# Moving the tiles of a decoder kernel to other bytes of the partition: parts of weights, keys and values at byte 64 modulo 128, parts of activations at byte 0

## The chip, the cores and the metric

The kernel runs on one core of a Trainium2 chip. The metric is the device time of one execution in microseconds. Three runs of the kernel before took 1002.29, 1002.46 and 1003.86 us; their median, 1002.46 us, is the time to compare with.

## The reference

A trunk of two layers works on 256 tokens of width 1024, all in float32. Each layer is a mixer between two half-step SwiGLU blocks, with an RMS norm ahead of every part and one at the end:

```python
y = (silu(h @ w_gate) * (h @ w_up)) @ w_out                    # SwiGLU, four times; D_FF = 2816
u, v = split(gelu(h @ w_in)); y = (u * (W_s @ LN(v) + b)) @ w_out   # mixer of layer 0; width 2048
y = stick_breaking_attention(h @ w_q, k, v) @ w_o              # mixer of layer 1; 16 heads of 64
```

Keys and values (4 heads) are projected once, from the output of layer 0. Every product is a product of a weight with 256 columns of activations, and every weight is read from memory once.

## The kernel before, in words

Float32 accuracy is kept by splitting each operand of a product into two parts, a high one of type float32r and the low rest. `mm3` (lines 144 to 150) then issues three matmuls for each tile of 128x128 weights: low weight by high activation (L148), high weight by low activation (L149), high by high (L150). A matmul has a stationary operand of 128 columns, which is loaded into the array (LDWEIGHTS, PEld in the profile), and a moving operand, which streams past it. The load for a matmul goes on while the matmul ahead of it streams.

`Weights.run_to` loads a weight tile of 128x1024 (`raw`, L71), splits it on ScalarE (`whi`, L81) and VectorE (`wlo`, L83), and hands it on some steps later. The steps follow in program order on TensorE:

- In a SwiGLU block, tagged a, b, c, d in order, step `in j` makes two banks, `g` and `u`, of 48 matmuls each. The weight is stationary and `xnh`, `xnl` (the normalised activations) move, 256 columns. Step `out j` adds 48 matmuls to four banks `y`: weight stationary, `hh`, `hl` (the gated hidden parts) moving. There are 11 steps of each kind in a block, and `out` comes one or two steps behind `in`. In block d, `out` is turned round: `hh`, `hl` are stationary and the weight moves, 512 columns (bank `yo`).
- The mixer of layer 0 has `v` (weight moving, `xn` stationary), `uu` (like `in`), `mix` (plain float32) and `ys` (like `out`).
- The attention has `kT` and a second `v` from `xkh`, `xkl`; `q` from `xn`; `z` (keys `kz` moving, `qh`, `ql` stationary); `o` (values `vd` stationary, `a0`, `a1` moving); and `yo` with `oT` moving.

Between the steps stand short float32 matmuls: the norm's `columns` (L313) and `rows` (L327), and transposes (`pgain` L253, `xb` L819).

A tile's byte in the partition follows from the order in which the pools are opened. They lie one behind the other, and each slot is rounded up to 32 bytes. In `const` the one-column tile `eps` takes 32 bytes; the pool ends at byte 18976, which is 32 modulo 128. `act` follows with `xT`, `xnh`, `xnl`, `acc` (multiples of 128 bytes, so all at 32), `rT` (32 bytes) and `spare` (2572 bytes in 2592), which leaves 96 for `rawp`, `hip`, `lop` and `hp`: `raw`, `whi`, `wlo`, `hh`, `hl`, `a0`, `a1` and `qh`, `ql` all start at 96. Slices of these tiles step by multiples of 512 bytes, so a tile's place modulo 128 holds for every operand cut from it. The pool `att` opens at 0: `kz`, `vd`, `xkh`, `xkl` and `oT` (in the slots of `xkh`, `xkl`) are at 0.

Of the kernel before, what the change touches and what calls it, by code (L numbers as in the profile page):

```python
# [8 lines left out]
F32 = mybir.dt.float32  # L9
# [6 lines left out]
P = 128  # L16
T = 256
# [82 lines left out]
def trunk(  # L100
# [21 lines left out]
    x = x[0]  # L122
    out = out[0]

    const = ctx.enter_context(tc.tile_pool(name="const", bufs=1))
    act = ctx.enter_context(tc.tile_pool(name="act", bufs=1))
    rawp = ctx.enter_context(tc.tile_pool(name="rawp", bufs=7))
    hip = ctx.enter_context(tc.tile_pool(name="hip", bufs=9))
    lop = ctx.enter_context(tc.tile_pool(name="lop", bufs=9))
    hp = ctx.enter_context(tc.tile_pool(name="hp", bufs=4))  # L130
    scr = ctx.enter_context(tc.tile_pool(name="scr", bufs=8))
    small = ctx.enter_context(tc.tile_pool(name="small", bufs=3))
# [131 lines left out]
    acc = act.tile([P, T], F32, name="acc")  # L264
    rT = act.tile([P, 2], F32, name="rT")

    spare = act.tile([P, P + 1 + 2 * (T + 1)], F32, name="spare")
    rb = spare[:, :T]
    diag = spare[:, T : 2 * T].rearrange("p (n t) -> p n t", n=2)

# [18 lines left out]
            nc.scalar.activation(s, xT[:, d, :], AF.Square)  # L289
            nc.gpsimd.tensor_add(acc, acc, s)  # L290

    eps = const.tile([P, 1], F32, name="eps")
    nc.vector.memset(eps, RMS_EPS)

    def newton(o, root, v, w):
# [343 lines left out]

    att = ExitStack()  # L640
    at = att.enter_context(tc.tile_pool(name="att", bufs=1))
    kz = [at.tile([P, 4, 2, T], F32R, name=f"kz{p}") for p in "hl"]
    vd = [at.tile([P, 2, 4, 2, 64], F32R, name=f"vd{p}") for p in "hl"]
    xkh = at.tile([P, KC, T], F32R, tag="bigh", name="xkh")
    xkl = at.tile([P, KC, T], F32R, tag="bigl", name="xkl")
    for t in kz:
# [265 lines left out]
```

## Time and profile before

| | |
|---|---|
| median of 3 runs | 1002.46 us |
| profiled execution, its own time | 1004.4 us |
| its span, first to last instruction | 1002.7 us |
| TensorE busy / loads of weights busy | 982.3 us / 963.5 us |
| VectorE / ScalarE / GpSimd busy | 645.2 / 504.1 / 86.5 us |
| traffic from memory | 176.73 MB read, 177 GB/s over the span |

Matmuls overlap in the pipeline: the busy time of one (its "mean ns") is more than twice the distance from its start to that of the next. The pace of TensorE is read from starts, as the time between two instructions divided by the matmuls between them.

### The profile page before, as it was taken

Reading aid. Unit: us, or ns where it says so; the run is one execution under the profiler, and the core shown is the slowest. Engines: PE = TensorE matmul, PEld = TensorE weight load, DVE = VectorE, ACT = ScalarE, POOL = GpSimd, SP = SyncE. Lnnn points to the kernel's source line nnn. Section 1 sums busy time; section 2 is a strip of 40 time slices with the busy share of each in tenths; the row PEclk is TensorE's granted clock in tenths of the full one; section 3 lists DMA queues with packets and bytes.
Section 4 is the critical chain, followed back from the end, with each engine's and each line's share of the span. In section 5 each row is a group of like instructions: output and inputs, shape, how many; then the busy total and the mean of one; then the engine's idle time right before and its main releaser. Section 6 shows DMA issues by size and latency. Waiting matters only on the chain.

```text
span 1002.7 us, 19306 instructions
## 1 busy us (share of the span) xinstructions
PE 982.3 (98%) x8042; PEld 963.5 (96%) x8042; DVE 645.2 (64%) x823; ACT 504.1 (50%) x690; POOL 86.5 (9%) x126
## 2 busy tenths in 40 slices
PE   8999999999999999999999999999997899999996
PEld 8999999999999999999999999999997899999996
DVE  6864675675866775656569755555678775565644
ACT  6643434475544564444448444444487674444433
POOL 4000000020000300000003000000046320000002
PEclk9999999999999999999999999999999999999999
DMA  9966565647555455666564866665643346656511
GB/s 304 322 195 190 169 189 188 190 143 222 184 177 175 133 191 188 193 188 193 186 195 146 247 189 191 189 193 186 190 149 92 97 147 191 207 172 203 176 42 43
DMA packets 135208, 179.56 MB, mean 179 GB/s; under 512 B 5624, under 2 KB 119376, under 8 KB 135120
## 3 DMA queue, kind: packets, MB, share of 16 engines
q1 hardware_dynamic: 134768, 177.76, 56.7%
q8 instruction: 63, 1.03, 0.4%
q0 software_dynamic: 192, 0.52, 0.2%
q14 instruction: 25, 0.20, 0.1%
q10 hardware_dynamic: 160, 0.05, 0.0%
HBM read 176.73 MB, written 1.05 MB: 177 GB/s over the span
## 4 chain that ended last, share of the span: by engine, by line
PE 89%; DVE 5%; ACT 2%; issue 1%; DMA 1%; POOL 1%; SPq 0%; ACTq 0%; POOLq 0%; DVEq 0%
PE yo L148 2%; PE yo L150 2%; PE yo L149 2%; PE yb L148 2%; PE yb L150 2%; PE yb L149 2%; PE ud L148 2%; PE ud L150 2%; PE gd L148 2%; PE ud L149 2%; PE gb L148 2%; PE gd L150 2%; PE gd L149 2%; PE ub L148 2%; PE gc L150 2%; PE gb L150 2%
## 5 line engine op out<-in xcount | busy, mean ns | idle before, releaser
L81 ACT CAST whi<-raw 128x1024 fp32r<-128x1024 f32 (+1 forms) x333 | 342.7, 1045 | 391.0 <-issue 205.3
L83 DVE TENSOR_TENSOR wlo<-raw,whi 128x1024 fp32r<-128x1024 f32 (+1 forms) x333 | 402.1, 1225 | 200.9 <-ACT whi L81 200.0
L290 POOL TENSOR_TENSOR acc<-acc,sq 128x256 f32<-128x256 f32 x39 | 33.8, 867 | 387.5 <-ACT sq L289 385.6
L148 PE MATMUL ga<-xnh,wlo 128*128 128x256 f32 x176 | 50.1, 285 | 0.0
L148 PE MATMUL ya<-hha,wlo 128*128 128x256 f32 x176 | 49.9, 284 | 0.2 <-DVE xT L399 0.2
L148 PE MATMUL yc<-hhc,wlo 128*128 128x256 f32 x176 | 49.9, 284 | 0.1
L148 PE MATMUL yb<-hhb,wlo 128*128 128x256 f32 x176 | 49.9, 284 | 0.0
L149 PE MATMUL ga<-xnl,whi 128*128 128x256 f32 x176 | 49.3, 280 | 0.5 <-DVE xnl L277 0.5
L149 PE MATMUL ya<-hla,whi 128*128 128x256 f32 x176 | 49.7, 282 | 0.0
L148 PE MATMUL gd<-xnh,wlo 128*128 128x256 f32 x176 | 49.7, 282 | 0.0
L149 PE MATMUL yb<-hlb,whi 128*128 128x256 f32 x176 | 49.7, 282 | 0.0
L149 PE MATMUL yc<-hlc,whi 128*128 128x256 f32 x176 | 49.7, 282 | 0.0
L150 PE MATMUL yb<-hhb,whi 128*128 128x256 f32 x176 | 49.6, 283 | 0.0
L148 PE MATMUL ua<-xnh,wlo 128*128 128x256 f32 x176 | 49.1, 279 | 0.5 <-DVE wlo L83 0.5
L150 PE MATMUL ya<-hha,whi 128*128 128x256 f32 x176 | 49.4, 283 | 0.0
L150 PE MATMUL gd<-xnh,whi 128*128 128x256 f32 x176 | 49.4, 281 | 0.0
L150 PE MATMUL ud<-xnh,whi 128*128 128x256 f32 x176 | 49.4, 281 | 0.0
L148 PE MATMUL ud<-xnh,wlo 128*128 128x256 f32 x176 | 49.4, 281 | 0.0
L149 PE MATMUL ud<-xnl,whi 128*128 128x256 f32 x176 | 49.4, 281 | 0.0
L149 PE MATMUL gd<-xnl,whi 128*128 128x256 f32 x176 | 49.4, 281 | 0.0
L150 PE MATMUL yc<-hhc,whi 128*128 128x256 f32 x176 | 49.4, 283 | 0.0
L150 PE MATMUL ga<-xnh,whi 128*128 128x256 f32 x176 | 49.1, 279 | 0.0
(289 smaller groups left out, 3353.6 us busy)
## 6 DMA issues: line engine op xcount, KB each, us to landing
raw<-in_ffn_w_in_dram SPq DMA_DIRECT2D x176, 512.0 KB, 4.5
raw<-in_ffn_w_out_dram SPq DMA_DIRECT2D x88, 512.0 KB, 4.3
raw<-in_a_w_in_dram SPq DMA_DIRECT2D x32, 512.0 KB, 4.4
raw<-in_a_w_out_dram SPq DMA_DIRECT2D x16, 512.0 KB, 3.3
raw<-in_b_w_q_dram SPq DMA_DIRECT2D x8, 512.0 KB, 4.5
raw<-in_b_w_o_dram SPq DMA_DIRECT2D x8, 512.0 KB, 4.0
raw<-in_w_kv_dram SPq DMA_DIRECT2D x4, 512.0 KB, 4.0
xin<-in_x_dram SPq DMA_DIRECT2D x4, 256.0 KB, 4.9
```

What stands on the lines that cost most here:

```text
L81: ins = nc.scalar.copy(hi[:, cc], raw[:, cc])
L83: ins = nc.vector.tensor_sub(lo[:, cc], raw[:, cc], hi[:, cc].bitcast(F32))
L148: nc.tensor.matmul(o, al, bh, start=first, stop=False, skip_group_check=True)
L149: nc.tensor.matmul(o, ah, bl, start=False, stop=False, skip_group_check=True)
L150: nc.tensor.matmul(o, ah, bh, start=False, stop=last, skip_group_check=True)
L290: nc.gpsimd.tensor_add(acc, acc, s)
```

## The change

The work and its order stay as they are. Only places move, by padding:

```diff
+    def gap(name, size):
+        pool = ctx.enter_context(tc.tile_pool(name=name, bufs=1))
+        pool.tile([P, size // 4], F32, name=f"{name}t")
     const = ...
     act = ctx.enter_context(tc.tile_pool(name="act", bufs=1))
+    gap("gapw", 32)
     rawp = ...; hip = ...; lop = ...
+    gap("gaph", 64)
     hp = ctx.enter_context(tc.tile_pool(name="hp", bufs=4))
...
-    spare = act.tile([P, P + 1 + 2 * (T + 1)], F32, name="spare")
+    spare = act.tile([P, P + 1 + 2 * (T + 1)], F32, name="spare", padded_shape=[P, 672])
-    eps = const.tile([P, 1], F32, name="eps")
+    eps = const.tile([P, 1], F32, name="eps", padded_shape=[P, 32])
...
     at = att.enter_context(tc.tile_pool(name="att", bufs=1))
+    at.tile([P, 8], F32, name="gapk")
     kz = ...; vd = ...
+    at.tile([P, 16], F32, name="gapx")
     xkh = ...; xkl = ...
```

Nothing reads or writes the gaps. By the sizes, the start bytes modulo 128 become:

| tiles | before | after |
|---|---|---|
| `xT`, `xnh`, `xnl`, `acc` | 32 | 0 |
| `spare` | 64 | 32 |
| `raw`, `whi`, `wlo` | 96 | 64 |
| `hh`, `hl`, `a0`, `a1`, `qh`, `ql` | 96 | 0 |
| `kz`, `vd` | 0 | 64 |
| `xkh`, `xkl`, `oT` | 0 | 0 |
| `wsT`, `bias`, `vsb`, `u` of the first mixer | 0 | 32 |

So the distance from the moving operand to the stationary one, modulo 128, goes from 64 to 64 where `xn` meets a weight, from 0 to 64 where `hh`, `hl` meet a weight, and from 32 or 96 to 64 in `kT`, the second `v`, `z`, `o` and the attention's `yo`.

## Rows read from the trace of the kernel before

**Rows 1.** The page: busy time by engine, and the granted clock by slices.
```profile
PE 982.3 (98%) x8042; PEld 963.5 (96%) x8042; DVE 645.2 (64%) x823; ACT 504.1 (50%) x690; POOL 86.5 (9%) x126
PEclk9999999999999999999999999999999999999999
```

**Rows 2.** The page: the chain that ended last, by engine.
```profile
PE 89%; DVE 5%; ACT 2%; issue 1%; DMA 1%; POOL 1%; SPq 0%; ACTq 0%; POOLq 0%; DVEq 0%
```

**Rows 3.** Timeline, block c: start us, us, engine, line, operation, out<-in, shapes, count.
```profile
572.57 0.29 PE L148 MATMUL gc<-xnh,wlo 128*128 128x256 f32 x1
...
583.47 0.28 PE L148 MATMUL yc<-hhc,wlo 128*128 128x256 f32 x1
...
589.21 0.29 PE L148 MATMUL gc<-xnh,wlo 128*128 128x256 f32 x1
```

**Rows 4.** Timeline, block d.
```profile
838.01 0.28 PE L148 MATMUL gd<-xnh,wlo 128*128 128x256 f32 x1
...
849.32 0.39 PE L148 MATMUL yo<-whi,hld 128*128 128x512 f32 x1
...
854.76 0.28 PE L148 MATMUL gd<-xnh,wlo 128*128 128x256 f32 x1
```

**Rows 5.** Groups by line and form: busy us, mean ns of one | idle us before.
```profile
L150 PE MATMUL gc<-xnh,whi 128*128 128x256 f32 x176 | 48.6, 276 | 0.0
L150 PE MATMUL gb<-xnh,whi 128*128 128x256 f32 x176 | 48.7, 277 | 0.0
L150 PE MATMUL ua<-xnh,whi 128*128 128x256 f32 x176 | 48.9, 278 | 0.0
L150 PE MATMUL uu<-xnh,whi 128*128 128x256 f32 x128 | 35.7, 279 | 0.0
L150 PE MATMUL v<-whi,xnh 128*128 128x256 f32 x128 | 35.8, 279 | 0.0
L150 PE MATMUL q<-xnh,whi 128*128 128x256 f32 x64 | 17.9, 279 | 0.0
L150 PE MATMUL gd<-xnh,whi 128*128 128x256 f32 x176 | 49.4, 281 | 0.0
L150 PE MATMUL yc<-hhc,whi 128*128 128x256 f32 x176 | 49.4, 283 | 0.0
L149 PE MATMUL ys<-hls,whi 128*128 128x256 f32 x128 | 36.2, 283 | 0.0
L149 PE MATMUL yo<-wlo,hhd 128*128 128x512 f32 x82 | 31.9, 389 | 0.0
```

**Rows 6.** Timeline, block a: a step behind a transpose of gains.
```profile
75.89 0.27 PE L253 MATMUL pgain<-ident,rows 56*128 56x56 f32 x1
76.08 0.39 PE L148 MATMUL ga<-xnh,wlo 128*128 128x256 f32 x1
76.31 0.28 PE L149 MATMUL ga<-xnl,whi 128*128 128x256 f32 x1
...
87.50 0.28 PE L148 MATMUL ya<-hha,wlo 128*128 128x256 f32 x1
```

**Rows 7.** Timeline, attention: one step of `yo`, up to the next `z`.
```profile
766.59 0.28 PE L148 MATMUL yo<-oTh,wlo 128*128 128x256 f32 x1
...
769.41 0.28 PE L148 MATMUL z<-kzh,ql 128*128 128x256 f32 x1
```

**Rows 8.** Timeline, block d: sixteen transposes in a row.
```profile
830.78 1.91 PE L819 MATMUL xb<-ident,xT 128*128 128x128 f32 x16
```

**Rows 9.** Groups by line and form: the splits of weights.
```profile
L83 DVE TENSOR_TENSOR wlo<-raw,whi 128x1024 fp32r<-128x1024 f32 x331 | 400.8, 1228 | 200.9 <-ACT whi L81 200.0
L81 ACT CAST whi<-raw 128x1024 fp32r<-128x1024 f32 x331 | 341.5, 1047 | 390.8 <-issue 205.3 <-PE gb L150 41.4 <-PE gd L150 39.4
```

## The prediction, made before the changed kernel ran

> **What bounds the kernel now.** I read the busy times first. TensorE is busy for 982.3 of 1002.7 us and its clock was granted in full in all 40 slices; no other engine is above 65% [rows 1]. Then the chain of waits: 89% of it is TensorE [rows 2]. So the end is set by how fast one matmul follows the other. The busy time can't tell this, since matmuls overlap, so I read starts in the timeline next. The reader is to see that one and the same matmul, 256 columns of float32r, runs at three paces.
>
> - In block c a step `in` has 96 matmuls from 572.57 to 583.47: 10.90 us, 113.5 ns each. The step `out` behind it has 48 up to 589.21: 5.74 us, 119.6 ns each [rows 3].
> - In block d the same step `in` takes 11.31 us for its 96: 117.8 ns each. The 24 wide matmuls (512 columns) behind it take 5.44 us: 226.7 ns each [rows 4].
>
> The groups by line repeat this over the whole run: the duration of one is the pace plus some 163 ns, so 276 ns stands for 113, 281 for 118, 283 for 120 [rows 5]. Nothing else separates these groups: the shape, the clock and the number of loads are the same. What differs between `in` (113.5 or 117.8) and `out` (119.6) is where the operands lie: moving at 32 and stationary at 96 in the one, both at 96 in the other. A step `in` has two paces at one and the same placing. The first of block c follows a step `out` and takes 113.5. A step that follows a lone transpose takes 87.50 - 76.31 = 11.19 us for 95 matmuls, 117.8 ns [rows 6], and keeps that to its end. I read this as two streams out of the same memory, the running operand and the next weights, that meet or miss each other; the distance modulo 128 says how often, and with a distance of 64 there are two rhythms, of which a break in the stream picks one.
>
> **The change part by part.** No instruction is added, removed or moved in its queue; no semaphore is added. The gaps are not written. What changes is the pace of three sets of matmuls.
>
> *Steps `out` of blocks a, b, c and `ys`.* Twelve groups, 9 x 176 + 3 x 128 = 1968 matmuls, now at 119.6 ns [rows 3, 5]. Their distance goes from 0 to 64, the distance that `in` has. They can then take either rhythm of `in`: at 117.8 each saves 1.8 ns (3.5 us in all), at 113.5 it saves 6.1 ns (12.0 us). I take the middle, 115.65 ns, since the groups of `in` are spread over both [rows 5]: 1968 x 3.95 = 7.8 us.
>
> *The wide matmuls of block d.* 3 x 82 = 246 at 226.7 ns, distance 0 [rows 4, 5]. No row shows a wide one at another distance in a steady stream. If a wide one loses per weight load what a narrow one loses, the gain is between nothing and 6.1 ns: 0 to 1.5 us. I take half, 0.8 us.
>
> *Attention, distance 32 or 96.* `yo` with `oT`: 24 matmuls in 2.82 us, 117.5 ns [rows 7]. There are 192 of these, 48 in `kT`, 48 in the second `v`, and 48 narrow ones in `z` and `o`: 336. At `yo`'s pace for all, going to 117.8 costs 0.1 us and going to 113.5 gains 1.3 us. Middle: 0.6 us.
>
> *Steps `in`, `uu`, `v`, `q`.* 24 groups of 176 and 15 rounds of 64 (`uu` 384, `v` 384, `q` 192): 5184 matmuls. Their distance stays 64, both operands move down by 32 bytes. I take nothing. The bounds are wide, since these are two thirds of the work. From (mean - 276) / 5 in the groups [rows 5], the share at 117.8 is about 0.5 in block a, 0.2 in b, 0 in c, 1 in d, 0.6 in `uu`, `v`, `q`: some 2300 matmuls. If all these went to 113.5 the gain is 2300 x 4.3 = 9.9 us; if the other 2900 went to 117.8 the loss is 12.5 us.
>
> *The small float32 matmuls and other engines.* Norm columns, rows, transposes and `mix` are under 300 instructions; sixteen transposes in a row run at (1.91 - 0.27) / 15 = 109 ns with the stationary operand at 32 and the moving one at 96 [rows 8]. I cost their shift at nothing. `raw`, `whi` and `wlo` move together, so the splits keep their relative places; they take 400.8 us of VectorE and 341.5 of ScalarE [rows 9], hidden under TensorE. That cover would be gone only if each grew by half. A faster TensorE asks for weights 1% sooner, which both can give.
>
> *Sum.* 7.8 + 0.8 + 0.6 + 0 = 9.2 us. The profiled execution took 1004.4 us (span 1002.7, 1.7 around it), so its like would take 995.2 us. It lies 1.9 us above the median of the runs; against the median, 1002.46 - 9.2 = 993.3 us.
>
> One rule of the Trainium skill speaks against any of this. The trace first: matmuls of one shape go at 113.5, 117.8 and 119.6 ns in neighbouring steps [rows 3, 4]. The page "TensorE: Matmul & The Clock Gate", section "Part 2: What happens when you issue a matmul", says that TensorE has two independent read ports, so that loading the next weights takes no read bandwidth from the running matmul. By that rule the place would not matter and the time would stay 1002.5 us; the rows disagree, unless the paces have a cause that I do not see (a rival below).
>
> **The rivals.**
>
> *Slower: the slow rhythm is carried on.* In the kernel before, a step `out` at distance 0 forces its own beat, and the `in` behind it came out at 113.5 [rows 3]. With one distance everywhere nothing resets the rhythm: what a norm or a transpose leaves behind [rows 6] holds through `in` and `out` until the next break. Price if it holds everywhere: 2900 x 4.3 = 12.5 us lost in `in`, 3.5 us won in `out`: 9.0 us more, 1011.5 us. It decides at the first steps behind a norm (the third step of block b: 113 or 118). For it: in block d, whose wide steps stand between, every `in` stays at 117.8 [rows 4, 5]. Against it: breaks differ, and block c is fast throughout [rows 5]. If it holds in one block only, gains and losses nearly cancel and the time is about 997.
>
> *The fast rhythm everywhere.* If 0 and 64 admit only the rhythm of 113.5: 12.0 + 9.9 + 1.5 + 1.3 = 24.7 us, 977.8 us. For it: 113.5 is the commonest pace at this distance. Against it: distance alone did not settle it in block d.
>
> *No meeting at all.* Both operands then start at a multiple of 64 bytes, which none but attention's tiles did. If runs of 64 bytes are what the memory hands out, a moving operand at 32 touches one run more than at 0, and 113.5 isn't the floor. The nearest row below is the transposes' 109.2 ns [rows 8]: 1968 + 5184 + 336 = 7488 matmuls gain a further 4.3 ns, 32 us beside the 24.7: 945.6 us. Against it: `oT` moves at 0, and its steps take 117.5 [rows 7], though at distance 32. In a sentence by itself: the same page of the Trainium skill, section "Back-to-back issue gap", gives 262 cycles for 256 columns, an estimate of 109.2 ns, which would make the same time.
>
> *The place as such matters the other way.* If 0 and 64 bring the pace of 119.6 to all: 2900 x 6.1 + 2300 x 1.8 = 21.8 us more, 1024.3 us. No row speaks for it; none excludes it, for no float32r pair at 0 and 64 is in the trace.
>
> *Nothing happens.* The paces come from something else that the blocks differ in, such as the bank written or the slices' higher address bits: 1002.5 us. Against it: the three blocks a, b, c agree on 119.6 in `out`, whatever slots they use.
>
> **How the numbers follow.** Forecast, a mixture of the two rhythms: 0.40, its own range 986 to 1000. Fast everywhere 0.20 (972 to 985); no meeting 0.15 (940 to 965); slow rhythm carried on 0.15 (1000 to 1012); nothing 0.06; worse everywhere 0.04. About 0.2% is what a measurement of this kernel can tell from no change. Faster by more: nearly all of the forecast, the two fast cases, a little of the carried rhythm, 0.73. Same: 0.09. Slower: most of the carried rhythm and the worst case, 0.18. The range from 950 to 1011 leaves out the lower part of the no-meeting case, the top of the carried one and the worst one, some 0.15 in all. Likeliest time 993.3 us.
>
> **What would show each step.** In the groups by line, `out` of a, b, c and `ys` should leave 283 ns: at 276 to 281 the distance is the cause, still at 283 the first step is wrong. Wide `yo` should fall from 389 to between 383 and 389. `gd` at 276 would speak for the fast rhythm everywhere, `gc` at 281 for the carried one; means of 272 to 273 in any of them for no meeting. Splits, loads and queues should keep their times. The forecast is wrong if steps `out` keep 119.6, or if `in`, which I left alone, moves by more than 9 us in all.

## The result and the profile after

The changed kernel takes 1011.33 us (median of four runs, 1010.14 to 1012.31) where the kernel before, run beside it, takes 1003.16: a ratio of 1.0079, interval 1.0060 to 1.0097. It is slower by 0.8%, where 0.9% faster was forecast. The time is that of the first rival, the slow rhythm carried on (1011.5 us).

The page of the profile after, busy times, granted clock and chain, which answer to [rows 1, 2]:

```profile
PE 992.0 (98%) x8042; PEld 972.0 (96%) x8042; DVE 643.9 (64%) x823; ACT 504.1 (50%) x690; POOL 85.5 (8%) x126
...
PEclk9999999999999999999999999999998999999999
...
PE 91%; DVE 4%; ACT 2%; DMA 1%; issue 1%; POOL 1%; SPq 0%; ACTq 0%; POOLq 0%; DVEq 0%
```

TensorE is busy 9.7 us longer for the same 8042 matmuls, at the same clock (2.4 GHz, full in all slices but one); VectorE, ScalarE and GpSimd moved by less than 2 us. So the loss is pace, as the sums from start to start below bear out. The groups by line and form of after, against [rows 5] (the lines of `mm3` are now L156 to L158):

```profile
L158 PE MATMUL gc<-xnh,whi 128*128 128x256 f32 x176 | 49.1, 279 | 0.0
...
L158 PE MATMUL v<-whi,xnh 128*128 128x256 f32 x128 | 35.4, 277 | 0.0
...
L158 PE MATMUL gd<-xnh,whi 128*128 128x256 f32 x176 | 49.2, 279 | 0.0
...
L158 PE MATMUL yc<-hhc,whi 128*128 128x256 f32 x176 | 48.8, 279 | 0.0
...
L157 PE MATMUL ys<-hls,whi 128*128 128x256 f32 x128 | 35.7, 279 | 0.0
...
L157 PE MATMUL yo<-wlo,hhd 128*128 128x512 f32 x82 | 32.3, 394 | 0.0
```

`gc` went up from 276 and `yc` down from 283, to one value. The reader should not take the mean's last digit for the pace (`gd` fell from 281 to 279 at the same pace); starts decide. The timeline of after in block c and in block d, answering to [rows 3, 4]:

```profile
574.67 0.28 PE L156 MATMUL gc<-xnh,wlo 128*128 128x256 f32 x1
...
585.98 0.28 PE L156 MATMUL yc<-hhc,wlo 128*128 128x256 f32 x1
...
591.63 0.28 PE L156 MATMUL gc<-xnh,wlo 128*128 128x256 f32 x1
...
844.08 0.28 PE L156 MATMUL gd<-xnh,wlo 128*128 128x256 f32 x1
...
855.39 0.39 PE L156 MATMUL yo<-whi,hld 128*128 128x512 f32 x1
...
860.99 0.28 PE L156 MATMUL gd<-xnh,wlo 128*128 128x256 f32 x1
```

Block c: 11.31 us for 96 matmuls of `in` (117.8 ns, before 113.5) and 5.65 us for 48 of `out` (117.7, before 119.6). Block d: `in` as before, 11.31 us; the 24 wide ones 5.60 us, 233.3 ns each, where they took 226.7. Summed from start to start over both whole traces:

| steps | before, us | after, us | change |
|---|---|---|---|
| `in` of a, b, c, d | 490.5 | 500.4 | +9.9 |
| `out` of a, b, c and `ys` | 238.0 | 234.5 | -3.6 |
| wide, block d | 56.0 | 57.5 | +1.5 |
| `uu` and `q` | 71.1 | 72.3 | +1.2 |
| both `v`, `kT`, `z`, `o`, narrow `yo` | 109.4 | 107.3 | -2.1 |
| float32 | 28.4 | 28.8 | +0.3 |

That is +7.3 us beside +6.8 in the spans (1002.7 to 1009.5).

### The profile page after: what moved, and what is told of

Its sections match the earlier page's. It is cut to its first block, busy times and chain, and to the rows that moved or that the text cites. A ratio compares the mean times of both kernels' runs of the same rounds, so it can differ in the third digit from the quotient of the medians.

```text
span 1009.5 us, 19306 instructions
## 1 busy us (share of the span) xinstructions
PE 992.0 (98%) x8042; PEld 972.0 (96%) x8042; DVE 643.9 (64%) x823; ACT 504.1 (50%) x690; POOL 85.5 (8%) x126
## 4 chain that ended last, share of the span: by engine, by line
PE 91%; DVE 4%; ACT 2%; DMA 1%; issue 1%; POOL 1%; SPq 0%; ACTq 0%; POOLq 0%; DVEq 0%
PE yo L156 2%; PE yo L158 2%; PE yo L157 2%; PE gc L156 2%; PE uc L156 2%; PE ub L158 2%; PE gb L158 2%; PE ud L156 2%; PE gc L158 2%; PE ub L157 2%; PE gb L157 2%; PE uc L158 2%; PE gb L156 2%; PE gd L156 2%; PE ub L156 2%; PE uc L157 2%
## 5 line engine op out<-in xcount | busy, mean ns | idle before, releaser
L156 PE MATMUL ga<-xnh,wlo 128*128 128x256 f32 x176 | 50.4, 286 | 0.0
L156 PE MATMUL ua<-xnh,wlo 128*128 128x256 f32 x176 | 49.4, 281 | 0.5 <-DVE wlo L83 0.5
L156 PE MATMUL yc<-hhc,wlo 128*128 128x256 f32 x176 | 49.5, 281 | 0.1
L156 PE MATMUL ya<-hha,wlo 128*128 128x256 f32 x176 | 49.5, 281 | 0.2 <-DVE xT L407 0.2
L156 PE MATMUL gd<-xnh,wlo 128*128 128x256 f32 x176 | 49.5, 281 | 0.0
L156 PE MATMUL gc<-xnh,wlo 128*128 128x256 f32 x176 | 49.5, 281 | 0.0
L156 PE MATMUL gb<-xnh,wlo 128*128 128x256 f32 x176 | 49.4, 281 | 0.0
L156 PE MATMUL yb<-hhb,wlo 128*128 128x256 f32 x176 | 49.4, 281 | 0.0
L158 PE MATMUL ga<-xnh,whi 128*128 128x256 f32 x176 | 49.3, 280 | 0.0
L156 PE MATMUL uc<-xnh,wlo 128*128 128x256 f32 x176 | 49.3, 280 | 0.0
L158 PE MATMUL gb<-xnh,whi 128*128 128x256 f32 x176 | 49.3, 280 | 0.0
L158 PE MATMUL ub<-xnh,whi 128*128 128x256 f32 x176 | 49.3, 280 | 0.0
L156 PE MATMUL ud<-xnh,wlo 128*128 128x256 f32 x176 | 49.2, 280 | 0.0
L158 PE MATMUL ua<-xnh,whi 128*128 128x256 f32 x176 | 49.2, 279 | 0.0
L158 PE MATMUL gd<-xnh,whi 128*128 128x256 f32 x176 | 49.2, 279 | 0.0
L156 PE MATMUL ub<-xnh,wlo 128*128 128x256 f32 x176 | 49.1, 279 | 0.0
L158 PE MATMUL ud<-xnh,whi 128*128 128x256 f32 x176 | 49.1, 279 | 0.0
```

The source lines that it names most:

```text
L156: nc.tensor.matmul(o, al, bh, start=first, stop=False, skip_group_check=True)
L158: nc.tensor.matmul(o, ah, bh, start=False, stop=last, skip_group_check=True)
```

## The experiments

Each kernel was timed beside the kernel before on the same chip, except the three bare streams, which ran once, with a profile. Bytes are places in the partition, worked out from the order and sizes of the tiles. Modulo 256 the distance (moving minus stationary) has a sign: in before it is 32 - 96, that is 192, in `in`, and 0 in `out`; in after it is 128 - 64 = 64 in both.

**h_at_64.** After, with the second gap behind `hp` and not ahead of it: h goes back to 64, `out` to distance 0, and `in` stays as in after.

```diff
-    gap("gaph", 64)
     hp = ...
+    gap("gaph", 64)
```

> The changed kernel with hh and hl (and a0, a1, qh, ql) at 64 in place of 0, all else in its new place. Carried rhythm (my theory): with distance 0 the steps out of blocks a, b, c take 119.6 to 120 ns again (group mean 283) and hand a fresh beat to the steps in, which go back to 113.3 ns in blocks b and c (276); the wide yo of block d back to 226.7 (389). About the time of the kernel before, 1000 to 1005 us. Rival, the place as such (0 and 64 slow, 32 and 96 fast): in stays at 117.8 (280) and out is at 120, some 1014 us. Rival, something else that the padding moved (scratch, norms): 1011 us, in at 117.8.

Measured: 1014.91 us, ratio 1.0105 (1.0091 to 1.0119). Block c:

```profile
578.61 0.28 PE L156 MATMUL gc<-xnh,wlo 128*128 128x256 f32 x1
...
589.92 0.29 PE L156 MATMUL yc<-hhc,wlo 128*128 128x256 f32 x1
...
595.68 0.28 PE L156 MATMUL gc<-xnh,wlo 128*128 128x256 f32 x1
```

`out` is back at 120 ns (5.76 us for 48) but `in` stays at 117.8 (11.31 for 96), in all 30 steps at 64 that follow one at distance 0 undisturbed; before has 28 such steps to 192, all fast. That a step `out` at distance 0 resets `in` to the fast rhythm fell as a general rule: it does so in before and not here, with the same distances modulo 128.

**h_only.** Before, with h alone moved by 64 bytes, from 96 to 32 modulo 128.

```diff
+    gap = ctx.enter_context(tc.tile_pool(name="gaph", bufs=1))
+    gap.tile([P, 16], F32, name="gapht")
     hp = ...
+    gap = ...                                  # "gaps", 64 bytes more
+    gap.tile([P, 16], F32, name="gapst")
     scr = ...
```

The second gap brings all that lies behind h to 128 bytes further on, the same place modulo 128.

> The kernel before with hh, hl, a0, a1, qh, ql alone moved, from 96 to 32, so that every pair of a weight and an activation is 64 apart, with x at 32 and weights at 96 as before. Carried rhythm: the same loss as with the whole change, in of blocks b and c at 117.8 (280), out at 117.8 (280), wide yo 233 (394): 1007 to 1013 us. Rival, the place as such: in of blocks b and c keeps 113.3 (276), out at 113 to 118: 985 to 1000 us.

Measured: 1001.27 us (999.56 to 1006.21), ratio 0.9978 (0.9953 to 1.0002), no difference that can be told, and outside both forecasts. The profiled execution was the longest of the four. Blocks b and c:

```profile
369.93 0.28 PE L152 MATMUL yb<-hhb,wlo 128*128 128x256 f32 x1
...
375.58 0.28 PE L152 MATMUL gb<-xnh,wlo 128*128 128x256 f32 x1
...
386.47 0.28 PE L152 MATMUL yb<-hhb,wlo 128*128 128x256 f32 x1
...
588.74 0.28 PE L152 MATMUL gc<-xnh,wlo 128*128 128x256 f32 x1
...
600.04 0.28 PE L152 MATMUL yc<-hhc,wlo 128*128 128x256 f32 x1
```

`out` 117.7 (5.65 for 48), `in` 113.4 in block b and 117.7 in block c. In block b the rhythm changes at the boundary of `out` and `in`, though by modulo 128 nothing changes there. Modulo 256 it does: `in` is at 192, `out` at 160 - 96 = 64.

**stream.** Matmuls alone, no other engine at work, at every distance and at five pairs of places with distance 64 modulo 128.

> No model at all, its output is not the reference's: a bare stream of float32r matmuls, 96 at a time, with no other engine at work, at moving-minus-stationary distances 0, 16, ... 112, each once behind 48 matmuls at distance 0 (names ending in r) and once behind two one-column float32 matmuls as a norm has them (ending in c); then distance 64 at five pairs of places, and 512 columns at 0, 32, 64, 96. Carried rhythm: distance 64 runs at 113.3 ns behind distance 0 and at 117.8 behind the break, at every pair of places alike; distance 0 at 120 either way. Rival, the place as such: the pairs 96/32 and 32/96 differ from 64/0 and 0/64. Rival, traffic of the other engines makes the slow pace: all of distance 64 at 113.3 or below, since nothing else runs.

The timeline (start, us, ..., count): streams of 96, each with a norm's columns or rows in its middle. In the names m is the moving operand's place and s the stationary one's, or d the distance with s at 0; the moving tile itself begins at 128 modulo 256.

```profile
144.76 11.47 PE L92 MATMUL d64r<-mv,st 128*128 128x256 f32 x96
156.07 0.50 PE L100 MATMUL cols<-ones,acc 128*128 128x1 f32 x4
156.44 11.15 PE L92 MATMUL d64c<-mv,st 128*128 128x256 f32 x96
...
288.01 11.47 PE L92 MATMUL m32s96r<-mv,st 128*128 128x256 f32 x96
...
299.56 11.66 PE L92 MATMUL m32s96c<-mv,st 128*128 128x256 f32 x96
```

Both rhythms appear with nothing else running (d64r 117.8 ns, d64c 113.3 by the starts), so neither needs traffic of other engines. The order is the reverse of the expected one, d64r behind distance 0 slow and d64c behind the break fast. No distance gave less than 113.3. The two pairs that are at 64 modulo 256 (m32s96, m0s64) were slow in four stretches of four; those at 192 (d64, m96s32, m64s0, m80s16) were fast in five of eight.

**breaks.** A stream at 192, interrupted.

> Also a bare stream, output not the reference's. Each trial starts with 48 matmuls at distance 0 and 24 at distance 64 (pre), then a break: 1 to 6 one-column float32 matmuls (c1x ... c6x), 1 or 2 float32 ones of 256 columns (r), 1 to 8 transposes (t), and then 48 at distance 64. Carried rhythm: pre at 113.3; behind a break either 113.3 or 117.8, kept to the end of the 48, by the kind and number of the break. The second part asks how many matmuls at distance 0 (s1x ... s36x) or at 32 or 96 (q) bring a stream at 117.8 back to 113.3: I expect 6 to 12 at distance 0. Rival: the rhythm goes back by itself within the 48, or a break does not change it at all.

```profile
205.77 0.50 PE L100 MATMUL cols<-ones,acc 128*128 128x1 f32 x4
206.13 3.07 PE L92 MATMUL p1x<-mv,st 128*128 128x256 f32 x24
209.04 0.29 PE L92 MATMUL same<-mv,st 128*128 128x256 f32 x1
209.17 5.63 PE L92 MATMUL s1x<-mv,st 128*128 128x256 f32 x48
214.63 5.86 PE L92 MATMUL same<-mv,st 128*128 128x256 f32 x48
```

The columns of a norm turned the fast stream slow (p1x: 24 in 2.91 us, first one included), and so in 19 of 19 times; in stream the same columns had turned the slow d64r into the fast d64c, so the kind of break alone does not say which rhythm it leaves. One matmul at another distance (`same`, 128 modulo 256) turned it fast again (s1x: 48 in 5.46 us, 113.8 with a few longer intervals at its head), and so did each of the nine longer runs of `same`, where 6 to 12 were thought to be needed. What a break leaves holds to the next.

**sign.** The same with both signs.

> A bare stream of TensorE (no part of the kernel's result; it leaves all of the computation out): 256-column matmuls whose moving operand lies 64 bytes below its stationary one in the partition (distance 192 modulo 256, streams m) or 64 bytes above it (distance 64, streams p), each entered from a stream at distance 0 and interrupted by ten kinds of break. Theory, the distance counts modulo 256: the m streams enter at 113.3 ns in most cases and the p streams at 117.8 in most, the change from m to p or back leaves a visible irregular interval, and distances 64 and 192 differ in the list of all distances as well as 32 and 160 or 96 and 224. Rival, the distance counts modulo 128 and the entry falls by the phase of the moment: m and p enter fast equally often (within 2 of 6 for the six lengths), and the list repeats after 128. In the wide streams the theory gives 226.7 ns at distance 0 alone and 233.3 at 64, 128 and 192; by the rival 128 has what 0 has.

```profile
25.68 4.41 PE L93 MATMUL m0r<-mv,st 128*128 128x256 f32 x36
...
408.63 6.64 PE L93 MATMUL d0r<-mv,st 128*128 128x256 f32 x54
...
427.23 6.53 PE L93 MATMUL d64r<-mv,st 128*128 128x256 f32 x54
...
445.83 6.58 PE L93 MATMUL d128r<-mv,st 128*128 128x256 f32 x54
...
464.32 6.31 PE L93 MATMUL d192r<-mv,st 128*128 128x256 f32 x54
...
482.60 6.99 PE L93 MATMUL w0r<-mv,st 128*128 128x512 f32 x30
...
492.30 7.17 PE L93 MATMUL w64r<-mv,st 128*128 128x512 f32 x30
```

Half of it came true. The distance counts modulo 256: 0 runs at 120.0 ns throughout, 128 at 118.8 with intervals from 115 to 122; 192 at 113.3, 64 at 117.8; wide ones at 226.7 for 0, 232.3 for 128, 233.3 for 64 and 192. But the m streams entered slow, 16 of 16, as did 15 of the 16 p streams. Behind the ten kinds of break 7 of 10 were fast at 192 and 3 of 10 at 64; and where m went over into p directly, each of the six kept its rhythm, three of them the fast one at 64. The m streams came to 192 by moving the *stationary* operand up; d192r, and `in` behind `out` in before, come to it by moving the *moving* one. The distance alone does not decide; no run here says why.

**w_at_192 and h_192.** All places modulo 128 as in after, the weights' parts at 192 modulo 256; and h_only with h 128 bytes further on. Both have distance 192 in `in` and in `out`. The edit of w_at_192, against after:

```diff
-    gap("gapw", 32)
-    gap("gaph", 64)
+    gap("gaph", 192)
-    spare = act.tile(..., padded_shape=[P, 672])
+    spare = act.tile(...)
```

> After, with every place modulo 128 as it is there, but the weights' parts moved by 128 modulo 256 (byte 192 in place of 64): the distance is 192 modulo 256 in both the in and the out steps, where it was 64. Theory (modulo 256; a place of 192 likes the fast rhythm): no irregular interval at the boundaries, each block keeps the rhythm with which it leaves the norm before it, and at least two of the four blocks run at 113.3 ns throughout; a block is worth (1056 + 528) x 4.45 ns = 7.0 us, all 6816 narrow steps 30 us, so 981 if all are fast, 997 if two are. Rival (modulo 128 is all that counts, and the slow rhythm is simply carried on): in and out of all blocks at 117.8 ns, 1011.3 +- 1.5 us.

> Before, with hh and hl 192 bytes on (place 32 modulo 256) where the earlier run h_only had them 64 bytes on (place 160, the same modulo 128): the distance is 192 modulo 256 in both in and out steps, where h_only had 192 and 64. Theory (modulo 256): the transients of h_only at every boundary between in and out are gone, each block runs in one rhythm from the norm before it to its end, mostly the fast one: 113.3 ns in in and out of at least two blocks, 977 us if in all, 984 with one slow block, 991 with two. Rival (modulo 128): as h_only, a new rhythm at each boundary, 1001 us (999 to 1006), out near 117.8 ns.

Measured: 998.46 us, ratio 0.9917 (0.9884 to 0.9951), ten runs from 988.15 to 1005.38 (1002.88 without the longest); and 997.34 (997.21 to 998.46), ratio 0.9930 (0.9915 to 0.9945). Groups of w_at_192:

```profile
L157 PE MATMUL gb<-xnh,whi 128*128 128x256 f32 x176 | 49.5, 281 | 0.0
...
L157 PE MATMUL gc<-xnh,whi 128*128 128x256 f32 x176 | 48.6, 276 | 0.0
L157 PE MATMUL yc<-hhc,whi 128*128 128x256 f32 x176 | 48.3, 276 | 0.0
```

One block is slow from end to end and the next fast, `in` and `out` alike: with one distance the rhythm is carried through a block. 128 bytes that leave every place modulo 128 alone took after from 1011 to 998. The two fast blocks that both forecasts asked for were not reached: in the profiled execution of either kernel c alone is fast throughout, and h_192 came out above its 977 to 991. The runs of w_at_192 lie 14.7 us apart without the longest, which would fit a rhythm picked anew in each execution, but was not traced; those of h_192 lie 1.3 us apart.

**after_rows2.** After, with the float32 matmul of the norm's rows issued twice.

> After, with the matmul of the norm's rows issued twice (one more fp32 matmul of 256 columns, 0.43 us, in five norms: 2.2 us); places as in after. In the bare stream two such matmuls were left in the fast rhythm (113.3 ns) where one was left in the slow. Theory 1 (a break picks the rhythm, and where the distance does not change it is carried to the next break): blocks b and c leave their norms fast and keep it, -7.0 us each, the first four steps of a -2.3, d's in steps -4.7; with the 2.2 us added about 992 us (986 to 1000). Theory 2 (at a distance of 64 modulo 256 the breaks of the kernel end in the slow rhythm, whatever they are): 1011.3 + 2.2 = 1013.5 us, in and out at 117.8 ns throughout.

Measured: 1014.73 us (1008.27 to 1016.92), ratio 1.0088 (1.0057 to 1.0119).

```profile
L158 PE MATMUL gc<-xnh,whi 128*128 128x256 f32 x176 | 49.1, 279 | 0.0
...
L158 PE MATMUL gb<-xnh,whi 128*128 128x256 f32 x176 | 48.6, 276 | 0.0
L158 PE MATMUL yb<-hhb,whi 128*128 128x256 f32 x176 | 48.5, 276 | 0.0
```

Block b alone went fast and stayed so: from start to start its `in` and `out` took 180.8 us, in after 187.2. So a distance of 64 can hold the fast rhythm, and after's pace is not a bound of its places; it is seldom picked there. Theory 2 has the time, theory 1 one block of four.

**after_reset, w192_reset, h192_reset.** One matmul at distance 0 behind each break, in after, w_at_192 and h_192.

```diff
+            if n == 0 and W.again:          # set by the norms, the extras, mix and back
+                w = ws[0][2][0]
+                nc.tensor.matmul(outs[0][:, :T], w[:, 0, :P], w[:, 1, :], start=True, stop=True, ...)
+                W.again = False
```

> After, with one matmul of 256 columns at distance 0 (a weight slice times the next, overwritten at once by the first true matmul) ahead of the first in step behind each break: 19 of them, some 0.15 us each, 2.9 us. From it the moving operand moves up by 64 bytes, to a distance of 64. Theory (the sign counts: from distance 0 the moving operand's step to +64 ends slow, as in h_at_64): nothing is won, 1011.3 + 2.9 = 1014 us, 117.8 ns in all steps. Rival (any change of the distance lets the stream fall into the fast rhythm, and it is carried from there): in and out of all four blocks at 113.3 ns, 1011.3 - 28 + 2.9 = 986 us.

> w_at_192 (the weights' parts at 192 modulo 256, all places modulo 128 as in after) with the same 19 matmuls at distance 0; here the moving operand moves down by 64 bytes behind them, as it does in before from out to in. Theory: it ends fast as there, and is carried, since in and out have one distance: 113.3 ns in both from ga_4 on, in b, c and d. Of the profile of w_at_192 (1000.85 us) 12 to 15 us go and 2.9 come: 988 us (983 to 992), and the runs scatter less than its 988 to 1005. Rival (the rhythm behind a break falls by chance, whatever the step is): as w_at_192 with 2.9 more, 1001 us (990 to 1008).

> h_192 (before with h 192 bytes on, the distance 192 in in and out) with the same 19 matmuls at distance 0. Theory: 113.3 ns in in and out from ga_4 on and in b, c and d; of 997.3 us 10 to 13 go and 2.9 come: 988 us (984 to 992). Rival (a chance at each break): 1000 us (996 to 1005).

Measured: 1014.29 (ratio 1.0089, 1.0056 to 1.0122), 991.83 (0.9899, 0.9865 to 0.9934) and 996.20 us (0.9915, 0.9899 to 0.9932). w192_reset beats both kernels and came within 4 us of its forecast; h192_reset came out 8 above its own, in the rival's range, with its block b slow. In after_reset, where all steps were to stay slow, block c was fast in the profiled execution (1008.08 us, the shortest of the four). Directly behind a float32 break the added matmul is no sure cure.

**after_every, w192_every.** The same matmul ahead of every projection, most of them in the midst of a stream.

> After with one matmul at distance 0 ahead of every projection (57 of them, 0.13 to 0.14 us each, 7.7 us), most of them in the midst of an undisturbed stream; behind it the moving operand steps up by 64 bytes, to distance 64. Theory (the step from 0 to 64 ends slow, whatever the rhythm was): every in and out step at 117.8 ns, 1011.3 + 7.7 = 1019 us (1017 to 1021). Rival (either rhythm by chance at each re-pick, whatever the sign): half of the 55 steps of 144 matmuls fast, -17 us, 1002 us. Second rival (a distance of 0 always sets the stream free): all fast, 985 to 990 us.

> The same 57 matmuls in w_at_192, where the step goes down, from distance 0 to 192 modulo 256; all places modulo 128 are those of after_every. Theory (that step ends fast, as from out to in in before): every in and out step at 113.3 ns, whatever the break ahead of it picked; v stays at 117.8; from w192_reset (profile 991.4 us) the slow steps of block a and the mix go, -5.6 us, and 38 more matmuls come, +5.1: 991 us (988 to 993), and the executions lie within 2 us of each other, where those of w_at_192 lay 17 apart. Rival (chance): half of the steps slow, 1007 us, spread over 5 us or more.

Measured: 1019.04 us (1018.50 to 1019.22; ratio 1.0148, 1.0131 to 1.0165) and 1000.35 (994.93 to 1002.14; 0.9951, 0.9931 to 0.9971). The timeline of after_every, block a, where a norm had for once left the fast rhythm (L423 is the added matmul):

```profile
35.80 0.28 PE L156 MATMUL ya<-hha,wlo 128*128 128x256 f32 x1
...
41.23 0.28 PE L423 MATMUL ga<-whi 128*128 128x256 f32 x1
...
52.66 0.28 PE L156 MATMUL ya<-hha,wlo 128*128 128x256 f32 x1
...
58.32 0.29 PE L423 MATMUL ga<-whi 128*128 128x256 f32 x1
```

`out` takes 5.43 us (113 ns); then the one matmul at distance 0; then `in` takes 11.3 us (117.8) and `out` 5.66 (117.9). The step from 0 up to 64 ended the fast rhythm for good. Over the trace 41 of 41 such steps end slow, though 28 of these streams had been slow at 64 already. In w192_every 39 of 41 steps from 0 to 192 end fast, and 29 had been fast at 192 already. What tells most are the nine steps of each that stand behind the wide matmuls of block d: all nine slow in after_every, all nine fast in w192_every, where w_at_192 has them all slow without it (h_192 all fast). One of w192_every (L422 is the added matmul; 10.89 us for 96):

```profile
849.04 0.28 PE L422 MATMUL gd<-whi 128*128 128x256 f32 x1
849.16 0.29 PE L155 MATMUL gd<-xnh,wlo 128*128 128x256 f32 x1
...
860.05 0.39 PE L155 MATMUL yo<-whi,hld 128*128 128x512 f32 x1
```

With the 30 slow steps of h_at_64 beside the 28 fast ones of before, the sign decides, with few exceptions, where a step from distance 0 ends when the moving operand makes it. That one added matmul turns a slow stream at 192 fast is not shown: in w192_reset and w192_every it did in two cases of five. The time of w192_every was not as forecast (1000, not 991, and a spread of 7 us), since what lies directly behind float32 breaks, in block a and the mixer, stayed mixed while 57 matmuls were paid for.

## Why the prediction was wrong

The price of before's fast `in` was known and the wrong case taken. Counted from the starts in the twelve traces of whole kernels (before, after and the ten here), over all stretches of 24 or more narrow matmuls with one distance: at a distance of 64 modulo 256 whatever interrupts the stream (a start more than 150 ns behind the last) leaves the slow rhythm in 192 of 200, at 192 in 112 of 242; a step from distance 0 ends slow in 78 of 79 at 64, and fast in 80 of 85 at 192. (A direct step between 64 and 192, most of them in h_only, is in neither count: it ended slow in 33 of 41 at 64 and in 24 of 41 at 192.) Before lives on the steps from 0 to 192, 28 of 28 in it. Its block b shows it, in rows beside those of [rows 3]: behind the norm's rows (L327) `in` takes 11.49 us for 96 matmuls, the first of them long, at the slow rhythm; then comes `out` at distance 0, 5.76 us; then `in` at the fast one, 10.91 us:

```profile
358.62 0.59 PE L327 MATMUL pstf<-spare,ones 128*128 128x256 f32 x2
358.86 0.47 PE L148 MATMUL gb<-xnh,wlo 128*128 128x256 f32 x1
...
370.35 0.28 PE L148 MATMUL yb<-hhb,wlo 128*128 128x256 f32 x1
...
376.11 0.29 PE L148 MATMUL gb<-xnh,wlo 128*128 128x256 f32 x1
...
387.02 0.28 PE L148 MATMUL yb<-hhb,wlo 128*128 128x256 f32 x1
```

Block c left its norm in the fast rhythm, without an `out` ahead of it (192 matmuls in 21.97 us, the first of them long):

```profile
544.86 0.47 PE L148 MATMUL gc<-xnh,wlo 128*128 128x256 f32 x1
...
566.83 0.28 PE L148 MATMUL yc<-hhc,wlo 128*128 128x256 f32 x1
```

Point by point:

- *`out` and `ys`, -7.8 us by "I take the middle".* Measured -3.6. The cause was right, they left 119.6 ns; the rhythm was not a mixture but the slow one throughout, the lower bound of 3.5 us.
- *`in`, `uu`, `v`, `q`, 0 us by "I take nothing".* This is the step that failed: `in` alone cost 9.9 us, `uu` and `q` 1.2. The text said that the distance "stays 64" and that both operands "move down by 32 bytes". By the sizes `xn` went up by 96 bytes and the weights by 224, which is down by 32 modulo 128 for both, but 128 bytes apart modulo 256: by sign the distance went from 192 to 64. The 9.9 us are also more than the 9 us that the prediction had named as a sign of being wrong. It also counted the steps of before as two pools at large, where most of those in the fast rhythm hung on the `out` ahead of them.
- *Wide, -0.8 us.* Measured +1.5, outside both bounds. Distance 0, where they were, was the best that any run shows; the bound "between nothing and 6.1 ns" carried the narrow ones' loss at distance 0 over to wide ones, which have none there (in sign 226.7 at 0, 233.3 at 64 and 192; in the kernels 226.7 and 228.2 at 0, 228.9 to 229.8 at 64, 232.8 to 233.5 at 192).
- *Attention, -0.6 us.* Its steps and `v` of layer 0, which the text had put with `in`, gave -2.1 together; the larger part is this `v`, six of whose eight steps fell into the fast rhythm (mean 277, was 279 [rows 5]).
- *The carried rhythm, chance 0.15.* Right in place and price: behind the norm of block b the third step runs at 117.8, and all of c with it; 1011.5 forecast, 1011.3 measured. That the two agree to 0.2 us is in part luck: its sum was +9.0 us, where the steps give +7.3 and the medians of the runs lie 8.2 apart, and it left out what the wide matmuls lost and `v` won. Its reason was half right. Nothing resets the rhythm when the distance is the same everywhere; but h_at_64, which brought the reset back, did not bring back the fast rhythm, so the sign bears a share that the rival did not have. The argument against it, that block c of before is fast throughout, did not count against it: c left its norm fast by itself, as the rows above show, and a rhythm that is carried would have kept it so. In after, at distance 64, the same norm left c slow; it is block b that the reset explains.
- *Fast everywhere, no meeting, nothing, worse everywhere.* Every `in` of blocks b, c and d in after runs at 117.8, none at 113.3 or 119.6, and no narrow stream went below 113.3 ns, bare or not. By the Trainium skill, "TensorE: Matmul & The Clock Gate", "Part 2", the next weights load over a port of their own and take no read bandwidth from the running matmul. By that rule the place would not matter; bare streams that differ in place alone take from 113.3 to 120.0 ns, so it does, though no run shows that the load of weights is what costs the time.

Open: why a step of the stationary operand to 192 ends slow (16 of 16) and one of the moving operand fast; which breaks leave which rhythm at 192; and what makes the two rhythms. That the running operand and the next weights "meet or miss each other", as the prediction read the paces, was never shown.

## What to carry to other kernels

Where TensorE sets the end, read the pace from starts, step by step, and ask of a fast step what ran ahead of it: a rhythm may be inherited, and a change that evens things out may take away what set it. Before costing a moved tile at nothing, work out the operands' distance with its sign and for a longer period than the one that seems to fit, and test it on a stream whose operands step as those of the kernel do. Give a bistable term both of its ends as cases, not their mean.

## What the runs showed of the hardware

The pace of one matmul shape at full clock depends on the two operands' places: 120.0 ns at distance 0 modulo 256, 113.3 or 117.8 at 64 and 192, 116.7 to 120.0 at the others tried, for 256 columns of float32r (stream and sign); wide ones the other way round, 226.7 to 228.2 ns at 0 and 228.9 to 234.4 elsewhere. One foreign matmul can switch a stream between its two rhythms for as long as it goes on: from fast to slow at 64 (41.23 us in after_every), from slow to fast at 192 (s1x in breaks), though not each time. The executions of one program lay 14.7 us apart (w_at_192, the longest left out), which would fit such a switch; the rhythms of each execution were not traced.
